# Three instructions reordered in an expert's closing sum, a ranking advanced by two steps, and an early load of a count

## The chip, the core and the metric

The kernel runs on one core of a Trainium2 chip. The core has five engines that each work through their own instructions in order: TensorE (PE in the profile; PEld is its weight load), VectorE (DVE), ScalarE (ACT), GpSimd (POOL) and SyncE (SP). They meet only at semaphores. SP and POOL issue most of the DMAs. The metric is the device time of one execution in microseconds (us); lower is better.

## The reference

One block of a hybrid decoder, on x of 1 x 4096 x 1024 in float32:

```python
h = rms_norm(x, attn_norm)
proj = h @ w_in                              # one projection for two groups of heads
o_a = gated_delta_net(...)                   # 4 heads, chunks of 64 tokens
o_b = retention(...)                         # 4 heads, chunks of 64 tokens
x = x + concat(o_a, o_b) @ w_out
h2 = rms_norm(x, ffn_norm)
x = x + hierarchical_moe(h2, ...)            # top 1 of 8 groups, then top 2 of its 8 experts
return rms_norm(x, final_norm)

# an expert, for the tokens routed to it (64 experts, hidden width 256):
y = (silu(t @ w_gate) * (t @ w_up)) @ w_down   # weighted by p(group) * p(expert | group)
```

Every token goes to two experts. Its row of the output is x plus both weighted results, normed with `final_norm`.

## The kernel before

The program has three stages. `mixer`, to about 2000 us, runs the projection and both groups of heads over eight blocks of 512 tokens. `post`, to about 2537 us, makes the output projection per block of 128 tokens (`Out.half`, L554 to L586), turns each finished block and routes its tokens (`turn_x`, and the generator `route`). The expert stage, 2537 to some 3470 us, runs the 64 experts.

The order of the instructions is that of the code: several generators are advanced in turns by hand. `side` is the list of side work in `post`. What stands in it there is `classes` (L1322 to L1370): from the counts of the first 28 of the 32 blocks it ranks the experts (VectorE, 64x64 tiles), so that the weights of the first four in the order can be fetched early. It yields between its steps: the counts (L1329, L1330), the groups' sizes (L1336 to L1344), their order (L1346 to L1354), the places (L1315 to L1318), a one-hot matrix `oh` (L1360 to L1364), and two small TensorE products with `oh` and `q` (L1367, L1368), whose results are `pe` and `br` (L1369, L1370). `turn_x` advances it by one step each time that a group of blocks has been handed to its routing; other places advance it too.

In the expert stage, round e of a Python loop runs the steps of several experts, in an order given as a string of letters, `LOOP = "AFCDNBEGIMHJLO"`; two rounds behind the last use `TAIL`. In a round, c is expert e, p the one before it (e-1) and q the one before that (e-2). The steps that matter here:

- F gathers for p the rows of the output that are so far there (`gather_y`, L1598, GpSimd's DMA).
- C and I are the gate and up matmuls of c (L1652), N the tanh of c (L1661, ACT).
- D is `sum_up` of q: for each of its tiles add (L1606, VectorE: `ys` plus the gathered row), square (L1611, ACT, which also sums over the row), rms (L1615 VectorE, L1616 GpSimd), gain (L1619, ACT: the row of `final_norm` times a flag of the token, plus 1).
- B and H turn the tiles of the next expert (L1582 TensorE, L1584 VectorE).
- E is silu of p: L1666 and L1667 (VectorE: `h`), L1668 (ACT: `hh`, the rounded high part), L1669 (VectorE: `hl`, the rest).
- G stores q: norm (L1623, L1624, VectorE, with the gain row `g`) and scatter (L1627, GpSimd's DMA).
- M scales the gathered rows of a later expert (L1575, ACT). J splits c's down weights into high and low parts (L1468 ACT, L1469 VectorE).
- O is the down projection of p: for each tile of up to 128 tokens two banks of 512 columns, six matmuls each (L975 to L977), each bank evicted by ACT into `ys` (L1595). The PSUM pool of these banks holds two, so the third bank of an expert with two tiles waits for the first eviction.

An expert has one tile or two, by its place in the order: 100 tiles in 64 experts. Flags and row numbers come from small tables (`mf`, `mi`). For a token's first expert the flag leaves the gain at 1, for its second it makes the final norm. A last loop, `For_i` over K (L1764), handles tokens beyond an expert's capacity; K is loaded into a register of five engines (L1763), and is 0 with these inputs.

The tiles `ys` and `g` (128 x 1024, float32) have two buffers each. The square's full-size result isn't used, only its sum; it is written into `g`, which gain then overwrites.

Of the kernel before, what the change touches and what calls it, by code (L numbers as in the profile page):

```python
# [8 lines left out]
F32 = mybir.dt.float32  # L9
# [3 lines left out]
AF = mybir.ActivationFunctionType  # L13
# [4 lines left out]
P = 128  # L18
D = 1024
# [9 lines left out]
NEXP, NGRP, EPG, DE = 64, 8, 8, 256  # L29
# [35 lines left out]
def pool(tc, ctx, name, bufs, **kw):  # L65
    return ctx.enter_context(tc.tile_pool(name=name, bufs=bufs, reuse_waits="tile", **kw))
# [845 lines left out]
NOV = 128  # L912
# [102 lines left out]
def post(tc, out, wrg, wre, sh, tab, then):  # L1015

    nc = tc.nc
    NR = out.x.shape[-2] // P
    with ExitStack() as ctx:
        cp, ap, sp = (pool(tc, ctx, n, b, side="right") for n, b in (("c1", 1), ("a1", 2), ("s1", 2)))  # L1020
# [12 lines left out]
        with tc.manual_schedule():  # L1033
            r0 = out.r
            if not out.mT:
                load_m(0)
                load_m(1)
                load_x(0)
                out.turn(0)
            load_x(r0 + 1)  # L1040

            back = [0, min(2 * r0, NR - NT)]
            xT, rst, scat, pend, side, again = [None], {}, [], [], [], {}
            turned = [0]

            def reload(end):
                while back[0] < min(back[1], end, turned[0] + 2):
                    r = back[0]
                    back[0] += 1
                    again[r] = y_row()  # L1050
                    nc.sync.dma_start(again[r], out.x1[r * P:(r + 1) * P, :])

            reload(r0)
            usb, oneb = (cp.tile([P, P], BF, name=n) for n in ("usb", "oneb"))
            oacc = cp.tile([P, 64], BF, name="oacc")
            nc.gpsimd.memset(oacc, 0.0)
            oaf = cp.tile([P, 64], F32, name="oaf")
            nc.gpsimd.memset(oaf, 0.0)
            sh.load()
            wrr = cp.tile([P, KC, 72], F32, name="wrr")  # L1060
            nc.sync.dma_start(wrr[:, :, 0:8], rows(wrg, 0, [[8, P], [P * 8, KC], [1, 8]]))
            nc.sync.dma_start(wrr[:, :, 8:72], rows(wre, 0, [[64, P], [P * 64, KC], [1, 64]]))
            load_m(r0 + 2)
            load_x(r0 + 2)
            wr = Split(cp.tile([P, KC, 72], F32R, name="wrh"), cp.tile([P, KC, 72], F32R, name="wrl"))

            def prepare():
                sh.prepare()
                yield
                nc.vector.tensor_copy(usb, C[:, C2_US:C2_US + P])  # L1070
                nc.vector.tensor_copy(oneb, C[:, C2_ONE:C2_ONE + P])
                for k in range(KC):
                    if k % 4 == 0:
                        yield
                    nc.vector.tensor_scalar(wrr[:, k], wrr[:, k], sh.pc[:, k:k + 1], None, op0=OP.mult)
                nc.scalar.activation(wr.hi, wrr, AF.Copy)
                yield
                nc.vector.tensor_tensor(wr.lo, wrr, wr.hi.bitcast(F32), op=OP.subtract)

            pend.append(prepare())  # L1080

            def on(gens):
                try:
                    return next(gens[0])
                except StopIteration:
                    gens.pop(0)

            def step():
                if pend:
                    on(pend)  # L1090
                if side and not older[0] in pend:
                    on(side)

            older = [None]

            def warm(n):

                t = out.ptr.tile([P, 4, P], F32, name="tr")
                for i in range(n):
                    nc.tensor.transpose(t[:, i % 4], sh.ident, sh.ident)  # L1100

            def turn_x(end):
                r = turned[0]
                if r >= end:
                    return
                turned[0] += 1
                i, sb = r % NT, r // NT
                if i == 0:
                    rst[sb] = [sp.tile([P, NT], F32, name=n) for n in ("ssq", "rst")]
                    xT[0] = Split(ap.tile([P, KC, T], F32R, name="xh", bufs=1), ap.tile([P, KC, T], F32R, name="xl", bufs=1))  # L1110
                if r < back[1]:
                    xi = again.pop(r)
                else:
                    xi = out.xi.pop(r)
                out.split_t(xi, xT[0].hi, xT[0].lo, slice(i * P, i * P + P))
                jx = ap.tile([P, D], BF, name="jx", bufs=1)
                nc.scalar.activation(jx, xi, AF.Square, accum_out=rst[sb][0][:, i:i + 1])
                reload(end)

                n = 2 if sb == NR // NT - 1 else NT  # L1120
                if (i + 1) % n == 0:

                    while pend and not (on(pend) and r == NR - 1):
                        pass
                    sl = slice(i + 1 - n, i + 1)
                    part = Split(*(t[:, :, sl.start * P:sl.stop * P] for t in (xT[0].hi, xT[0].lo)))
                    new = (route(tc, (r + 1 - n) * P, n, out.x.shape[-2], sh, (rst[sb][0][:, sl], rst[sb][1][:, sl]), part,
                                      wr, usb, oneb, oacc, oaf, tab, scat, (out.pacc, out.ptr, out.psm, sp)))
                    next(new)
                    while pend:  # L1130
                        on(pend)
                    pend.append(new)
                    if side:
                        on(side)
                    if sb == NR // NT - 2:
                        older[0] = new
                        side.append(classes(tc, sh, oneb, oacc, out.psm, sp))

            if NR == NT:
                side.append(classes(tc, sh, oneb, oacc, out.psm, sp))  # L1140
            for r in range(r0, NR):
                for i in out.half(r, 0):
                    if not i and r + 1 < NR:
                        out.turn(r + 1)
                    step()
                reload(r)
                for i in out.half(r, 1):
                    n = turned[0]
                    if not i or n < r:
                        turn_x(r)  # L1150
                    if n == turned[0] or turned[0] % NT and (turned[0] < NR - NT or turned[0] % 2):
                        step()
                load_m(r + 3)
                load_x(r + 3)
            while side:
                on(side)
            then()
            while turned[0] < NR:
                reload(NR)
                turn_x(NR)  # L1160
            on(pend)
            warm(40)
            while pend:
                on(pend)
            rank(tc, sh, oneb, oacc, out.psm, sp, warm)
            warm(140)
# [261 lines left out]
def moe(tc, w_gate, w_up, w_down, sh, x1, tab, info, out):  # L1428

    nc = tc.nc  # L1430
# [6 lines left out]
    with ExitStack() as ctx:  # L1437
        wp = pool(tc, ctx, "w2", 2)
        C, ident, pc, fn, ex, rk, pm, ovi = sh.C, sh.ident, sh.pc, sh.fn, sh.ex[:, 0:1], sh.rk, sh.pi, sh.ovi
# [50 lines left out]
        cp, ap, sp = (pool(tc, ctx, n, b) for n, b in (("c2", 1), ("a2", 2), ("s2", 2)))  # L1490
# [65 lines left out]
        class Rows:  # L1556
# [50 lines left out]

            def square(self):
                self.ss = sp.tile([P, 2], F32, name="ss2", bufs=4)
                self.g = ap.tile([P, D], F32, name="g")  # L1610
                nc.scalar.activation(self.g, self.xg, AF.Square, accum_out=self.ss[:, 0:1])  # L1611

            def rms(self):
                ss = self.ss
# [1 line left out]
                nc.gpsimd.tensor_tensor(ss[:, 1:2], ss[:, 0:1], ex, op=OP.pow)  # L1616

            def gain(self):
                nc.scalar.activation(self.g, fn, AF.Copy, scale=self.col(SEC), bias=1.0)  # L1619

            def norm(self):
# [72 lines left out]
        with tc.manual_schedule():  # L1694
# [23 lines left out]
            new(2)  # L1718
            X[1].each("scale")
            for e in range(NEXP + 2):  # L1720
                c, n, m, p, q = (X[i] if 0 <= i < len(X) else None for i in (e, e + 1, e + 2, e - 1, e - 2))
                if e % G == 0 and e + G < NEXP:
                    pend = table(batch(e + G))

                def sum_up():
                    for t in q.tiles:
                        t.add()
                        t.square()
                        t.rms()
                        t.gain()  # L1730

                def store():
                    for t in q.tiles:
# [24 lines left out]
                for o in LOOP if e < NEXP else TAIL:  # L1758
                    do, f = steps[o]
                    if do:  # L1760
                        f()

        K = nc.values_load(ovi[0:1, 2 * NOV:2 * NOV + 1], min_val=0, max_val=NOV)  # L1763
        with tc.For_i(0, K, 1) as j:  # L1764
            w = Weights(ovi[0:1, bass.ds(j, 1)])
            w.index()
# [18 lines left out]
            x.tanh()  # L1785
            x.silu()
            x.down()
            for f in ("gather_y", "add", "square", "rms", "gain", "norm", "scatter"):
                x.each(f)


# [49 lines left out]
```

## Time and profile before

| | |
|---|---|
| Three runs | 3479.33, 3486.98, 3489.43 us; median 3486.98 |
| Profiled execution | 3483.95 us, span 3482.0 us |
| Mean granted TensorE clock | 0.993 |
| TensorE busy (PE / weight loads) | 3382.3 us (97%) / 3102.6 us (89%) |
| VectorE busy | 2160.8 us (62%) |
| ACT busy | 1492.9 us (43%) |
| GpSimd busy | 1010.6 us (29%) |

The shares are means over three unlike stages. A row of an engine's timeline, as used below, reads: start, duration, engine, line, operation, result and inputs, how many such instructions in a row (x). A bracket at its end gives the idle time of the engine just before it and whom that waited for. Starts of neighbours may lie closer than a duration, since instructions overlap at their ends.

### The profile page before, as it was taken

To read this page: it belongs to the slowest core of one execution; us is meant where nothing else is said; L and a number is where in the kernel's file an instruction comes from. 1 tells how busy PE (TensorE), PEld (TensorE's weight loads), DVE (VectorE), ACT (ScalarE), POOL (GpSimd) and SP (SyncE) were. 2 spreads that over 40 slices of the span, in tenths; PEclk is the share of its full clock that TensorE was granted. 3 is DMA by queue.
4 is the path that set the end of the run, shared out by engine and by line. 5 is a ranking of instruction groups with operands and counts; after the bars stand their busy time and mean duration, and the time that the engine had idled before them with its cause. 6 is when DMAs were issued, how large, how long until landed. Compare 5 with 4: busy or idle time off the path is not lost. (4 is left out here: it accounts for less than half of the span.)

```text
span 3482.0 us, 65321 instructions
## 1 busy us (share of the span) xinstructions
PE 3382.3 (97%) x24377; PEld 3102.6 (89%) x24377; DVE 2160.8 (62%) x5718; ACT 1492.9 (43%) x3322; POOL 1010.6 (29%) x1320
## 2 busy tenths in 40 slices
PE   7999999999999999999999999999999999999996
PEld 6989999999999999999999988888888888888885
DVE  5785576576467566656655734444556677767775
ACT  4444243233333333333332323222255667766775
POOL 1322222232232322322222211111224344444543
PEclk9999999999999999999999999999999999999998
DMA  8675445454544545454554444323378898999995
GB/s 270 225 247 183 162 159 197 159 190 170 182 168 169 179 150 201 159 179 166 181 183 162 145 156 137 123 102 110 132 230 289 285 312 294 311 323 333 336 320 189
DMA packets 393422, 710.98 MB, mean 204 GB/s; under 512 B 52704, under 2 KB 272528, under 8 KB 393104
## 3 DMA queue, kind: packets, MB, share of 16 engines
q1 hardware_dynamic: 356736, 622.03, 52.6%
q0 software_dynamic: 34976, 84.20, 6.7%
q8 instruction: 193, 3.16, 0.4%
q14 instruction: 125, 1.02, 0.1%
q10 hardware_dynamic: 1392, 0.56, 0.1%
HBM read 606.19 MB, written 131.99 MB: 212 GB/s over the span
## 5 line engine op out<-in xcount | busy, mean ns | idle before, releaser
L248 PE MATMUL acc<-wq,hh 128*128 128x256 f32 (+1 forms) x2560 | 744.7, 291 | 16.6 <-DVE gs L281 6.8
L250 PE MATMUL acc<-wq,hl 128*128 128x256 f32 (+1 forms) x2560 | 722.4, 282 | 1.8 <-DVE hl L326 1.8
L249 PE MATMUL acc<-wq,hh 128*128 128x256 f32 (+1 forms) x2560 | 723.2, 283 | 0.2 <-DVE wq L145 0.2
L248 PEld LDWEIGHTS acc<-wq,hh 128*128 128x128 f32 x2560 | 486.2, 190 | 23.8 <-DVE gs L281 9.0
L250 PEld LDWEIGHTS acc<-wq,hl 128*128 128x128 f32 x2560 | 484.5, 189 | 2.6 <-DVE hl L326 2.6
L249 PEld LDWEIGHTS acc<-wq,hh 128*128 128x128 f32 x2560 | 486.1, 190 | 0.7 <-DVE wq L145 0.7
L236 PE MATMUL acc<-hh,wq 128*128 128x512 f32 x768 | 317.7, 414 | 0.0
L238 PE MATMUL acc<-hh,wq 128*128 128x512 f32 x768 | 301.6, 393 | 0.0
L237 PE MATMUL acc<-hl,wq 128*128 128x512 f32 x768 | 301.0, 392 | 0.0
L1652 PEld LDWEIGHTS g<-xT,gu 128*128 128x128 f32 x2048 | 270.3, 191 | 13.2 <-DVE xT L1584 3.4
L1652 PE MATMUL g<-xT,gu 128*128 128x128 f32 (+30 forms) x2048 | 275.6, 293 | 1.5 <-DVE xT L1584 1.5
L1652 PE MATMUL u<-xT,gu 128*128 128x128 f32 (+30 forms) x2048 | 275.6, 293 | 0.0
L1652 PEld LDWEIGHTS u<-xT,gu 128*128 128x128 f32 x2048 | 265.9, 191 | 1.9
L274 DVE SCALAR_TENSOR_TENSOR cv<-xin,pcol,cv 128x512 f32<-128x512 f32 x288 | 216.4, 751 | 73.4 <-ACT cv L272 66.6
L282 POOL TENSOR_TENSOR gs<-gs,nrow 128x256 f32<-128x256 f32 x128 | 98.1, 766 | 448.1 <-DVE gs L281 413.7
L1627 POOL DMA_INDIRECT out_dram<-xg,mi x100 | 130.8, 1308 | 189.0 <-DVE ss L1623 96.4
L975 PE MATMUL y<-dh,hh 128*128 128x512 f32 (+16 forms) x400 | 164.5, 411 | 21.7 <-ACT ys L1595 13.9
L1595 ACT ACTIVATE ys<-y,mf 128x512 f32<-128x512 f32 (+22 forms) x200 | 134.0, 681 | 115.8 <-PE y L977 115.1
L849 POOL TENSOR_TENSOR rqk<-rqk,rb 128x256 f32<-128x256 f32 x128 | 115.3, 901 | 222.6 <-DVE rb L848 132.3
L1598 POOL DMA_INDIRECT xg<-out_dram,mi x97 | 100.5, 1036 | 263.8 <-PE tr L1582 48.4
L238 PEld LDWEIGHTS acc<-hh,wq 128*128 128x128 f32 x768 | 144.2, 188 | 33.0
L291 POOL TENSOR_TENSOR ss<-ss,ex 128x2 f32<-128x2 f32 x128 | 101.4, 792 | 236.8 <-DVE ss L290 203.7
(377 smaller groups left out, 7942.4 us busy)
## 6 DMA issues: line engine op xcount, KB each, us to landing
wq<-wsp SPq DMA_DIRECT2D x420, 512.0 KB, 5.8
gu<-in_w_gate_dram SPq DMA_DIRECT2D x128, 512.0 KB, 6.4
gu<-in_w_up_dram SPq DMA_DIRECT2D x128, 512.0 KB, 7.9
dn<-in_w_down_dram SPq DMA_DIRECT2D x64, 1024.0 KB, 9.5
xi<-in_x_dram SPq DMA_DIRECT2D x64, 512.0 KB, 5.0
wsp<-wq SPq DMA_DIRECT2D x60, 512.0 KB, 4.4
mixed<-mx SPq DMA_DIRECT2D x128, 128.0 KB, 2.7
xi<-mixed SPq DMA_DIRECT2D x32, 512.0 KB, 4.7
```

Of the source, the lines that this page charges most:

```text
L236: nc.tensor.matmul(a, wh[:, s], hh[:, k, :], start=(k == 0), stop=False)
L237: nc.tensor.matmul(a, wh[:, s], hl[:, k, :], start=False, stop=False)
L238: nc.tensor.matmul(a, wl[:, s], hh[:, k, :], start=False, stop=(k == KC - 1))
L248: nc.tensor.matmul(a[:, :n], hh[:, k, s], wh[:, :n], start=(k == 0), stop=False)
L249: nc.tensor.matmul(a[:, :n], hh[:, k, s], wl[:, :n], start=False, stop=False)
L250: nc.tensor.matmul(a[:, :n], hl[:, k, s], wh[:, :n], start=False, stop=(k == KC - 1))
L274: nc.vector.scalar_tensor_tensor(cv, xin[:, j:j + T], tap(j), cv, op0=OP.mult, op1=OP.add)
L849: nc.gpsimd.tensor_tensor(o.rearrange("p h s d -> p (h s d)"), o.rearrange("p h s d -> p (h s d)"), b.rearrange("p h s d -> p (h s d)"), o ...
L975: nc.tensor.matmul(out, a.hi, b.hi, start=(i == 0), stop=False)
L1595: nc.scalar.activation(self.y[:R, s], y[:R], AF.Copy, scale=self.f[:R, WT, self.n:self.n + 1])
L1627: so = nc.gpsimd.indirect_dma_start(out=orow, out_offset=self.idx(0), in_=self.xg[:self.G], in_offset=None, bounds_check=S - 1, oob_is_err ...
L1652: nc.tensor.matmul(o[:, b, :R], self.w.gu[k // 4][:, k % 4, i * DE + b * P:i * DE + b * P + P], self.xT[:, k, :R], start=(k == 0), stop=(k ...
```

## The change

Four edits, with no instruction added or removed on any engine. `sum_up` runs gain first, then add, square and rms; the square writes its unused result into `ys` (`self.y`, already read by the add) rather than `g`. The load of K moves from behind the two tail rounds to the head of the first of them. `turn_x` advances `classes` by two steps where it advanced it by one.

```diff
@@ turn_x
                     pend.append(new)
-                    if side:
-                        on(side)
+                    for _ in range(2):
+                        if side:
+                            on(side)
@@ class Rows
             def square(self):
                 self.ss = sp.tile([P, 2], F32, name="ss2", bufs=4)
-                self.g = ap.tile([P, D], F32, name="g")
-                nc.scalar.activation(self.g, self.xg, AF.Square, accum_out=self.ss[:, 0:1])
+                nc.scalar.activation(self.y, self.xg, AF.Square, accum_out=self.ss[:, 0:1])
@@
             def gain(self):
+                self.g = ap.tile([P, D], F32, name="g")
                 nc.scalar.activation(self.g, fn, AF.Copy, scale=self.col(SEC), bias=1.0)
@@ the rounds of the experts
             for e in range(NEXP + 2):
+                if e == NEXP:
+                    K = nc.values_load(ovi[0:1, 2 * NOV:2 * NOV + 1], min_val=0, max_val=NOV)
@@
                 def sum_up():
                     for t in q.tiles:
+                        t.gain()
                         t.add()
                         t.square()
                         t.rms()
-                        t.gain()
@@ behind the rounds
-        K = nc.values_load(ovi[0:1, 2 * NOV:2 * NOV + 1], min_val=0, max_val=NOV)
         with tc.For_i(0, K, 1) as j:
@@ in that loop
-            for f in ("gather_y", "add", "square", "rms", "gain", "norm", "scatter"):
+            for f in ("gather_y", "gain", "add", "square", "rms", "norm", "scatter"):
                 x.each(f)
```

Line numbers behind the first edit are higher by one in the changed kernel up to the loop over the experts, except where the edits themselves shift them.

ACT in the expert stage, at the first `sum_up` with two tiles, before (`xg_29727` and `xg_29728` are the gathered rows of the two tiles, `fn` the row of `final_norm`):

```order
L1595 ACTIVATE ys<-y,mf 128x512 x4
L1611 ACTIVATE g,ss_30386<-xg_29727 128x1024
L1619 ACTIVATE g<-fn,mf 128x1024
L1611 ACTIVATE g,ss_30393<-xg_29728 128x1024
L1619 ACTIVATE g<-fn,mf 128x1024
L1661 ACTIVATE h<-g 128x2x76
L1668 ACTIVATE hh<-h 128x512
```

The same place of the changed kernel:

```order
L1596 ACTIVATE ys<-y,mf 128x512 x4
L1620 ACTIVATE g<-fn,mf 128x1024
L1611 ACTIVATE ys,ss_30388<-xg_29727 128x1024
L1620 ACTIVATE g<-fn,mf 128x1024
L1611 ACTIVATE ys,ss_30395<-xg_29728 128x1024
L1662 ACTIVATE h<-g 128x2x76
L1669 ACTIVATE hh<-h 128x512
```

Each gain (L1619, now L1620) went ahead of its tile's square; a square now stands last before the tanh.

TensorE near the end of `post`, before: the last output projection (L576 to L578), the two products of `classes` (`sm`), and the turn of the last block (`xi_28621`):

```order
L576 MATMUL acc<-hh,mh 128x512
L577 MATMUL acc<-hl,mh 128x512
L578 MATMUL acc<-hh,ml 128x512
L1367 MATMUL sm<-oh,cst_24670 128x64
L1368 MATMUL sm<-cst_24670,q 128x64
L554 MATMUL tr<-id,xi_28621 128x128 x8
```

In the changed kernel the products stand right behind the turn of the block before the last (`xi_28472`):

```order
L554 MATMUL tr<-id,xi_28472 128x128 x8
L1368 MATMUL sm<-oh,cst_24670 128x64
L1369 MATMUL sm<-cst_24670,q 128x64
L576 MATMUL acc<-hh,mh 128x512
L577 MATMUL acc<-hl,mh 128x512
L578 MATMUL acc<-hh,ml 128x512
```

Twelve matmuls (four times L576, L577, L578), which stood ahead of the products, now stand behind them.

GpSimd at the end of the tail, before: scatters of the last three tiles, the last gather, the load of K (`ovi`) and the loop's branch:

```order
L1627 DMA out_dram<-xg_29727,mi 4096x1024
L1598 DMA xg_29729<-out_dram,mi 96x1024
L1616 TENSOR_TENSOR ss_39730<-ss_39730,ex_24671 128x1
L1627 DMA out_dram<-xg_29728,mi 4096x1024
L1616 TENSOR_TENSOR ss_39759<-ss_39759,ex_24671 128x1
L1627 DMA out_dram<-xg_29729,mi 4096x1024
L1763 TENSOR_LOAD ovi
L1764 COMPARE_AND_BRANCH
```

The same place of the changed kernel:

```order
L1628 DMA out_dram<-xg_29727,mi 4096x1024
L1723 TENSOR_LOAD ovi
L1599 DMA xg_29729<-out_dram,mi 96x1024
L1616 TENSOR_TENSOR ss_39746<-ss_39746,ex_24671 128x1
L1628 DMA out_dram<-xg_29728,mi 4096x1024
L1616 TENSOR_TENSOR ss_39775<-ss_39775,ex_24671 128x1
L1628 DMA out_dram<-xg_29729,mi 4096x1024
L1766 COMPARE_AND_BRANCH
```

The load went ahead of one gather and two scatters.

## Rows read from the trace of the kernel before

**Rows 1.** Expert stage: length, then busy PE, PEld, DVE, ACT, POOL; clock, DMA share, GB/s.

```profile
2537.00:3482.00 945.00, 896.62 (x6100) 788.72 (x6098) 649.84 (x1288) 630.49 (x855) 400.89 (x394) 0.99 0.87 295
```

**Rows 2.** Waits in the expert stage, TensorE: us in total, times, longest.

```profile
PE y L975 <- ACT ys L1595: 13.9, 15, 1.5
PE y L975 <- ACT hh L1668: 7.8, 9, 2.1
```

**Rows 3.** The same view, of VectorE and ACT.

```profile
DVE ss L1615 <- ACT g L1611: 142.8, 100, 2.7
...
ACT g L1611 <- DVE xg L1606: 82.8, 75, 6.0
...
ACT hh L1668 <- DVE h L1667: 63.1, 62, 2.8
...
DVE xg L1606 <- DMA xg<-out_dram,mi: 1.6, 2, 1.1
```

**Rows 4.** ACT's timeline in the round at 2586: first square, second gain, tanh.

```profile
2586.05 1.05 ACT L1611 ACTIVATE g<-xg 128x1024 f32<-128x1024 f32 x1
...
2589.72 1.15 ACT L1619 ACTIVATE g<-fn,mf 128x1024 f32<-128x1024 f32 x1
2590.78 0.28 ACT L1661 ACTIVATE h<-g 128x152 f32<-128x152 f32 x1
```

**Rows 5.** ACT's timeline in the round at 3410: first square, and `hh`.

```profile
3410.47 1.06 ACT L1611 ACTIVATE g<-xg 128x1024 f32<-128x1024 f32 x1 [2.89 <-DVE xg L1606]
...
3416.07 0.42 ACT L1668 ACTIVATE hh<-h 128x260 fp32r<-128x260 f32 x1 [0.52 <-DVE h L1667]
```

**Rows 6.** ACT and TensorE in the round at 3368: square, first `ys`, third bank.

```profile
3368.16 1.04 ACT L1611 ACTIVATE g<-xg 128x1024 f32<-128x1024 f32 x1
...
3378.35 1.50 ACT L1595 ACTIVATE ys<-y,mf 128x512 f32<-128x512 f32 x2
...
3379.07 0.39 PE L975 MATMUL y<-dh,hh 128*4 128x512 f32 x1
```

**Rows 7.** ACT and TensorE in the round at 2586: `hh`, down, `ys`, third bank.

```profile
2592.16 0.63 ACT L1668 ACTIVATE hh<-h 128x512 fp32r<-128x512 f32 x1 [1.10 <-DVE h L1667]
...
2592.97 0.48 PE L975 MATMUL y<-dh,hh 128*128 128x512 f32 x1
...
2596.67 1.24 ACT L1595 ACTIVATE ys<-y,mf 128x512 f32<-128x512 f32 x2
...
2597.39 0.50 PE L975 MATMUL y<-dh,hh 128*128 128x512 f32 x1 [1.26 <-ACT ys L1595]
```

**Rows 8.** ACT and TensorE in the round at 3105: `hh` and down.

```profile
3111.22 0.40 ACT L1668 ACTIVATE hh<-h 128x236 fp32r<-128x236 f32 x1 [0.72 <-DVE h L1667]
...
3113.30 0.49 PE L975 MATMUL y<-dh,hh 128*118 128x512 f32 x1
```

**Rows 9.** VectorE near the end of `post`: a residual add, and `oh`.

```profile
2487.50 0.69 DVE L583 TENSOR_TENSOR xi<-acc,xi 128x512 f32<-128x512 f32 x1 [2.49 <-PE acc L578]
...
2501.70 0.24 DVE L1364 TENSOR_SCALAR oh<-cst,q 64x64 f32<-64x64 f32 x1
```

**Rows 10.** TensorE there: the products of `classes`, and the last block's turn.

```profile
2502.00 0.43 PE L1367 MATMUL sm<-oh,cst 64*128 64x64 f32 x2 [2.31 <-DVE oh L1364]
...
2502.58 1.09 PE L554 MATMUL tr<-id,xi 128*128 128x128 f32 x8
```

**Rows 11.** TensorE up to the first expert: a gap in the routing, the first turn.

```profile
2515.06 0.19 PE L1265 MATMUL sm<-ob,usb 128*128 128x64 bf16 x1 [1.08 <-DVE ob L1260]
...
2536.51 0.75 PE L1582 MATMUL tr<-cst,xg 76*128 76x76 f32 x8 [0.91 <-ACT xg L1575]
```

**Rows 12.** The granted clock (third number from the end) after two gaps, as rows 1.

```profile
2504.00:2506.00 2.00, 1.76 (x7) 1.47 (x8) 1.97 (x10) 1.40 (x3) 0.00 (x0) 0.50 0.58 190
...
2516.00:2520.00 4.00, 3.24 (x26) 2.83 (x25) 3.47 (x26) 3.75 (x4) 1.50 (x2) 1.00 1.10 352
```

**Rows 13.** GpSimd's load of K: duration in ns (min, median, max), first and last start.

```profile
L1763 POOLq TENSOR_LOAD <-ovi x1: 502/502/502, 3465.7 to 3465.7; - x1
```

## Prediction

> **What bounds the kernel now.** I read the busy time by stage first [rows 1]. The expert stage, 2537 to 3482 us, holds all that three of the four edits touch; TensorE is busy there for 896.62 of 945 us and ACT for 630.49. TensorE sets the pace, so an edit counts only where TensorE waits, or comes to wait. The waits of TensorE in that stage [rows 2] show for whom: the down projection (L975) waits 13.9 us in 15 places for `ys`, ACT's eviction, and 7.8 us in 9 places for `hh`, ACT's rounding of the hidden tile. So the moments at which ACT finishes `hh` and `ys` matter. Then the waits of the lines that the reorder moves [rows 3]: ACT sat 82.8 us before 75 of the 100 squares until VectorE's add was done; VectorE sat 142.8 us before `rms` until the square was done; ACT sat 63.1 us before 62 of the 64 `hh` until VectorE had `h`. That gives the chain of one round: add (VectorE), square (ACT), `rms` (VectorE), for a second tile the same again, then the turn, silu, `h` (VectorE), `hh` (ACT), down (TensorE). VectorE runs in order and `rms` waits for the square, so the square sits on the chain to `hh`; the gain doesn't.
>
> **The order gain, add, square, rms.** Nothing is added or taken away; per tile, one ACT instruction of 1.15 us goes ahead of the square. Its price as a place in ACT's row is 1.06 us, start of gain 2589.72 to start of the next 2590.78 [rows 4]; I use 1.05.
> Two kinds of rounds follow. In an early round ACT comes to the square before the add is done: 2.89 us of waiting at 3410.47 [rows 5]. The gain fits into that wait, and the square starts when it did. What does this buy? ACT is free 1.05 us sooner behind the last square, but its next instruction on the chain is `hh`, for which it waits anyway (0.52 us at 3416.07 for `h`). VectorE's chain has not moved, so nothing is gained. The gain of a second tile moves into the place where the first one's stood, between the two squares: no change either.
> In a late round the add has long been done, and ACT comes straight from the last `ys` eviction to the square: the one at 2586.05 has no wait [rows 4], the one at 3368.16 has none [rows 6]. There the gain now stands in the way: square, `rms`, turn, silu, `h` and `hh` all come up to 1.05 us later, and with `hh` all that ACT does behind it (scale, `dh`, `ys`). I went through the 62 rounds that have a square and a later `hh`, by ACT's wait before the first square: 29 are late, 20 with no wait and 9 with 0.16 to 0.91 us. The delays (1.05 less the wait) add up to 25.2 us. How much of it reaches TensorE is read from the down projection of each:
> - In the round at 2586, down starts at 2592.97, 0.18 us after `hh` (2592.16 + 0.63), and its third bank waits for `ys` from 2596.67 already (1.26 us, [rows 7]). Both move with ACT: full cost, 1.05. Four more are like it (2648, 2711, 2916, 2960): 5 x 1.05 = 5.25.
> - In the round at 3368 TensorE doesn't wait yet, but the third bank (3379.07) starts just when the first half of `ys` at 3378.35, 0.70 us long, is done [rows 6]: about 1.0. The round at 3297 is alike, and the one at 3034 has a delay of 0.82: 2.82.
> - At 2798 and 2900 `ys` has some 0.39 us to spare: 2 x 0.66 = 1.32. At 3019, 3338 and 3424 it is 0.17, 0.39 and 0.06: 0.62.
> - The other 16 cost nothing. Either the expert behind has one tile, so that no third bank is wanted, and down starts long after `hh`: at 3105 `hh` ends at 3111.62 and down starts at 3113.30 [rows 8], 1.68 us to spare. Or ACT waits over a microsecond for TensorE before its first `ys`, which swallows the delay.
> Sum 5.25 + 2.82 + 1.32 + 0.62 = 10.0 us. After each such round ACT waits for TensorE or meets an early round, so delays don't pile up. From below: if the spare times were all larger than the records say, 0; if ACT's freed microsecond did reach `hh` and `ys`, minus half of the 21.7 us in [rows 2], some 11 us gained. From above: all 25.2. I take 10.0 because it is read round by round.
>
> **The square into `ys`.** Same instruction, same size; `ys` has two buffers and is next written by ACT itself, in order. It only holds `ys` until the square, and the next eviction stands behind that on the same engine: 0.
>
> **The classes two steps at once.** VectorE's 64x64 ranking, ending in `oh`, stood between the routing steps of the last blocks; `oh` came at 2501.70 [rows 9], and TensorE sat 2.31 us for it at 2502.00 [rows 10]. Now the six instructions of the first step come while VectorE waits for the output projection (2.49 us idle before 2487.50), and the next steps run one place earlier each. Adding up the durations in the new order gives `oh` at about 2497.5. TensorE wants it earlier too, at 2496.7, ahead of twelve matmuls instead of behind them, and waits 0.8. Then 0.58 us for the small products (2502.00 to 2502.58), 12 x 0.23 for the matmuls, and the residual add (0.69 us at 2487.50) before the next block's turn: this starts at about 2501.8, and its first half perhaps at 2501.0, where it was 2502.58. So about 1.0 us (0.75 to 1.5). Behind it, up to the first expert at 2536.51 [rows 11], TensorE only waits for routing, tables and gathers, and the dummy transposes fill the time; a shift there goes through to the end.
> The clock adds to it. After the 2.31 us gap the granted clock is 0.50 in 2504 to 2506 [rows 12], the 1.2 GHz level: half of 2 us, 1.0 us of full speed is lost there. It stays low a little beyond, but TensorE also waits a little in this window, so I leave it at 1.0. After a gap of 1.08 us (2515.06, [rows 11]) the clock is 1.00 [rows 12]. The new gaps are no longer than that one, so I take the 1.0 as saved. The Trainium skill ("TensorE: Matmul & The Clock Gate", "What's actually happening") puts it thus: the throttled level is the default and activity releases it; the trace agrees so far as the low clock follows the longest gap. Together -2.0, bounds 0 to -2.6 (1.5 for the turn, 1.1 for the clock).
>
> **The load of K.** Five engines load the count. Four did so in the tail beside their own running work; SyncE's moves to the end of its queue, where nothing waits. GpSimd's load, 0.50 us [rows 13], stood with the last scatter at the end of the chain; now it stands ahead of the last gather, where GpSimd is idle. The scatter was queued first, so the chain may only seem to pass through the load: 0 to -0.5, I take -0.2. If TensorE's or VectorE's load weren't covered by the last rounds' work, up to 0.5 each is lost.
>
> **The sum.** +10.0 - 2.0 - 0.2 = +7.8 us. The profiled run took 3483.95 us, the median of the three is 3486.98; between the two, 3485.5 + 7.8 = 3493.3, so 3493.
>
> **The rivals.**
> - ACT's order doesn't matter: the delays vanish in spare time that the records understate (ends of matmuls are modelled). For it: 33 rounds have room. Against it: 15 places where TensorE already waits for `ys`. Time: 3485.5 - 2.2 = 3483. The Trainium skill ("Perfetto Trace Analysis", "Identifying the Most-Contended Engine") would have one work on the engine with the highest occupancy first, and ACT is not that one; by this rule the reorder is nothing. The waits in [rows 2] speak against it.
> - The freed microsecond counts: filling 75 waits lets ACT run ahead, and `hh` and `ys` come sooner. Against it: 62 of 64 `hh` wait for `h`. Time: 3485.5 - 11 - 2.2 = 3472.
> - The delay goes all through (slower by far): a late square makes norm and scatter late, the scatter holds back the next `gather_y`, and the add of an early round starts late in turn. It decides from the point at which most gathers land after the engines are ready. Against it: so far the add waited for a gather only twice, 1.6 us in all [rows 3]. Time: 3485.5 + 25.2 - 2.2 = 3508.
>
> **How the numbers follow.** Forecast 0.57, with a range of its own of 3487 to 3499 (reorder +4 to +14, the rest 0 to -3); order doesn't matter 0.20; freed microsecond 0.06; delay all through 0.17. 0.3% is 10.5 us, about what can be told from no change: the bounds are 3476.5 and 3497.5. Slower by more: a fifth of the forecast (0.11) and nearly all of the last case (0.16), 0.27. Faster by more: the third case, and a little for the second, 0.07. The rest 0.66. The range, 3480 to 3506, leaves out most of the third case and the far half of the last.
>
> **What would show it.** ACT's wait for the add before the square falls from 82.8 to about 43 (33 early rounds by 1.05 each, the nine partly late ones by 5 in all); VectorE's wait for the square grows from 142.8 by about 25; TensorE's waits for `ys` and `hh` grow from 21.7 to about 32. If VectorE's wait grows and TensorE's doesn't, the first rival holds; if both fall, the second; if TensorE's grow by 20 or more, the third. TensorE's wait for `oh` shows 0.8, the clock stays at 1.00, and the first expert's turn starts some 2 us before 2536.51. No load of K stands in the chain's end. I am wrong if the late squares don't start later.

## The result and the profile after

| | before | changed |
|---|---|---|
| six runs each, median | 3485.01 us | 3504.65 us |
| lowest to highest | 3479.33 to 3489.43 | 3500.07 to 3508.43 |
| span of the profiled execution | 3482.0 us | 3505.7 us |

The ratio is 1.0054 (95% interval 1.004 to 1.0068): slower by 18.8 us (13.9 to 23.7). The forecast was 3493, its range 3480 to 3506. The sign was right and the time lies in the range, 1.4 us below its upper end, but the loss is more than twice the +7.8 of the sum.

The waits in the expert stage, over the whole of it (us in total, times, longest), answer to [rows 2, 3]:

```profile
DVE ss L1615 <- ACT ys L1611: 166.5, 99, 3.6
ACT hh L1669 <- DVE h L1668: 120.6, 63, 2.8
...
ACT ys L1611 <- DVE xg L1607: 46.3, 59, 3.6
...
PE y L975 <- ACT ys L1596: 18.7, 18, 1.5
PE y L975 <- ACT hh L1669: 14.9, 14, 3.1
...
PE g L1653 <- DVE xT L1585: 2.5, 6, 0.7
...
DVE xg L1607 <- DMA xg<-out_dram,mi: 2.1, 4, 1.3
```

ACT's wait for the add fell from 82.8 to 46.3 us, as the gain now fills it (43 was forecast). VectorE's wait for the square grew by 23.7 us (25 forecast). TensorE's waits for `ys` and `hh` grew from 21.7 to 33.6 us (32 forecast). So the delay is where it was looked for, and of the size in those rows. Yet the time grew by more than these 11.9 us.

Where the rest is, one stretch shows: from the first to the last turn of the expert stage, before (first row) and after (second), columns as in rows 1.

```profile
2536.50:3437.40 900.90, 877.71 (x5972) 773.16 (x5973) 631.35 (x1258) 612.72 (x829) 390.31 (x383) 1.00 0.90 306
```

```profile
2536.70:3461.20 924.50, 888.01 (x5972) 777.60 (x5973) 630.15 (x1258) 601.08 (x830) 396.82 (x383) 0.99 0.88 298
```

Of the 23.7 us by which the profiled execution is longer, 23.6 are here. TensorE's idle time (length less busy) went from 23.2 to 36.5 us, +13.3. And with the same 5972 matmuls it was busy 10.3 us longer. Part of that is the clock: over these two stretches, the granted clock lost 1.7 us against full speed before, in one place (within 3096 to 3102), and 8.5 us after, in three (within 2539 to 2547, 3112 to 3117 and 3436 to 3445; the shares of full speed lost there are 0.43, 0.34 and 0.38). That is 6.8 us more. The other 3.5 us or so I can't assign: the ends of matmuls are modelled, and weight loads that wait may stretch them.

The late round of [rows 4, 7]: the last `ys` ahead of the first square, before, and ACT in the changed kernel:

```profile
2585.47 0.69 ACT L1595 ACTIVATE ys<-y,mf 128x512 f32<-128x512 f32 x1 [0.67 <-PE y L977]
```

```profile
2588.94 0.69 ACT L1596 ACTIVATE ys<-y,mf 128x512 f32<-128x512 f32 x1 [0.61 <-PE y L977]
2589.53 1.14 ACT L1620 ACTIVATE g<-fn,mf 128x1024 f32<-128x1024 f32 x1
2590.57 1.04 ACT L1611 ACTIVATE ys<-xg 128x1024 f32<-128x1024 f32 x1
2591.61 1.14 ACT L1620 ACTIVATE g<-fn,mf 128x1024 f32<-128x1024 f32 x1
2593.12 1.06 ACT L1611 ACTIVATE ys<-xg 128x1024 f32<-128x1024 f32 x1 [0.37 <-DVE xg L1607]
2594.18 0.28 ACT L1662 ACTIVATE h<-g 128x152 f32<-128x152 f32 x1
2596.73 0.63 ACT L1669 ACTIVATE hh<-h 128x512 fp32r<-128x512 f32 x1 [2.28 <-DVE h L1668]
```

and TensorE behind it:

```profile
2597.41 0.50 PE L975 MATMUL y<-dh,hh 128*128 128x512 f32 x1 [0.76 <-ACT hh L1669]
...
2601.96 0.50 PE L975 MATMUL y<-dh,hh 128*128 128x512 f32 x1 [1.26 <-ACT ys L1596]
```

From the start of the last `ys` to that of the first square it is 1.63 us, where it was 0.58 (2585.47 to 2586.05): 1.05 later, exactly the gain's place. ACT then waits 2.28 us for `h` (1.10 before): the time that the early gain took is handed back as a wait that no one can use. Down waits 0.76 us where it had 0.18 to spare. The wait for `ys` is as long as before, 1.26 us, but comes later.

The end of `post`, TensorE, answers to [rows 10, 11]: the turn of the last block but one and the dummy transposes (L1100), before, then the changed kernel:

```profile
2495.92 1.03 PE L554 MATMUL tr<-id,xi 128*128 128x128 f32 x8
...
2509.45 4.53 PE L1100 MATMUL tr<-cst 128*128 128x128 f32 x40
```

```profile
2498.05 1.03 PE L554 MATMUL tr<-id,xi 128*128 128x128 f32 x8
...
2499.67 0.43 PE L1368 MATMUL sm<-oh,cst 64*128 64x64 f32 x2 [0.59 <-DVE oh L1365]
...
2503.12 0.60 PE L554 MATMUL tr<-id,xi 128*128 128x128 f32 x4
2504.06 0.66 PE L554 MATMUL tr<-id,xi 128*128 128x128 f32 x4 [0.35 <-DVE xi L583]
...
2509.47 4.53 PE L1100 MATMUL tr<-cst 128*128 128x128 f32 x40
```

The wait for `oh` is 0.59 us (2.31 before, 0.8 forecast), and the last turn now waits for the residual add, as the sum had it. From the one to the other it is 11.42 us, where it was 13.53: 2.1 us saved. The clock, last columns of two windows:

```profile
2504.00:2506.00 2.00, 1.29 (x11) 0.96 (x12) 0.91 (x3) 1.53 (x3) 0.00 (x0) 1.00 0.58 211
2506.00:2508.00 2.00, 2.00 (x18) 2.00 (x18) 1.97 (x15) 0.59 (x2) 0.00 (x0) 1.00 0.89 265
```

It stays at 1.00 where it was 0.50 in the first of them. The first expert starts at 2536.65, and not some 2 us before 2536.51 as forecast: this execution came to the turn of the last block but one 2.1 us later (2498.05 against 2495.92), and had been as late at 2195 us already, ahead of every edit.

### The profile page after: what moved, and what is told of

Read it like the earlier page. It is cut to its first block, busy times and chain, and to the rows that moved or that the text cites. A ratio compares the mean times of both kernels' runs of the same rounds, so it can differ in the third digit from the quotient of the medians.

```text
span 3505.7 us, 65421 instructions
## 1 busy us (share of the span) xinstructions
PE 3396.0 (97%) x24377; PEld 3110.7 (89%) x24377; DVE 2159.7 (62%) x5718; ACT 1479.9 (42%) x3322; POOL 1016.7 (29%) x1320
## 5 line engine op out<-in xcount | busy, mean ns | idle before, releaser
L248 PEld LDWEIGHTS acc<-wq,hh 128*128 128x128 f32 x2560 | 487.8, 191 | 22.3 <-DVE gs L281 9.1
L975 PE MATMUL y<-dh,hh 128*128 128x512 f32 (+16 forms) x400 | 165.7, 414 | 33.6 <-ACT ys L1596 18.7
```

Of the source, the lines that this page charges most:

```text
L248: nc.tensor.matmul(a[:, :n], hh[:, k, s], wh[:, :n], start=(k == 0), stop=False)
L975: nc.tensor.matmul(out, a.hi, b.hi, start=(i == 0), stop=False)
```

## The experiments

Each was timed beside the kernel before, on the same chip; us are the ratio times the median of before beside it (3484.06 for the first four, 3490.84 for the next four, 3489.48 for the last two).

**Only the order.** All of the diff but the `turn_x` loop and the move of K. 

> Only the order of sum_up (gain first, square into ys); classes and K as before. Theory A, the late square: the whole loss of the change (+18.8 us) and the 1 to 2 us that the other edits were to give back come from here, so +14 to +21 us, TensorE's waits for ys and hh about 34 us as in the changed kernel (21.7 before). Rival B, the classes edit costs the rest (it moved a stretch of low clock to 2538-2546 us, 3.3 us lost): +8 to +12 us here.

Measured: 1.0052 (1.004 to 1.0064), +18.1 us (13.9 to 22.3). TensorE's waits for `ys` and `hh` are 32.1 us in its trace. The reorder, with its square into `ys`, is the whole loss; rival B falls.

**Only the classes.**

```diff
-                    if side:
-                        on(side)
+                    for _ in range(2):
+                        if side:
+                            on(side)
```

> Only the classes two steps at once. Theory A: -2 to 0 us against before. Rival B: +3 to +8 us, with a stretch of low clock in the first expert's up matmuls (2538 us on).

Measured: 0.9995 (0.9986 to 1.0003), -1.7 us (-4.9 to +1.0). That suits the forecast's -2.0, but alone it can't be told from no change. Its trace does have a stretch of low clock at the first expert (2534.6 to 2541.4 us), as rival B had it, and the time is none the worse. In nine of the twelve traces of this case some such stretch begins between 2534 and 2553 us: in all three kernels with this edit, in six of the nine without it. So it doesn't need the classes. What does go with them is the stretch that the prediction counted: in all nine traces without this edit a low clock begins between 2499 and 2520 us, in the three with it none does.

**Gain first for pairs alone, and for single tiles alone.** Both with the square into `ys`.

```diff
                     for t in q.tiles:
+                        if len(q.tiles) == 2:     # the other kernel: == 1
+                            t.gain()
                         t.add()
                         t.square()
                         t.rms()
-                        t.gain()
+                        if len(q.tiles) == 1:     # the other kernel: == 2
+                            t.gain()
```

Pairs: 

> Gain first only in the rounds whose sum has two tiles; single tiles as before. All 29 late rounds of the trace of before have two tiles. Theory A: the same time as with the whole reorder (+14 to +21), since all late rounds are in it. Rival C, what costs is something that every tile has (the buffer ys held longer, or the gain waiting for a free g): about 0.7 of it, 72 of 100 tiles.

Measured: 1.0056 (1.004 to 1.0071), +19.5 us (13.9 to 24.7), as the whole reorder.

Single tiles: 

> Gain first only in the 28 rounds whose sum has one tile. Theory A: none of them is late (ACT waited 1.33 us or more for the add in each), the gain fits into the wait, and nothing waits for it: within 2 us of before, ACT's wait for the add about 25 us shorter. Rival C: about 0.3 of the whole reorder, +4 to +6. Rival D, freed ACT time counts: -4 us or more.

Measured: 1.0007 (0.9999 to 1.0016), +2.4 us (-0.3 to +5.6). ACT's wait for the add is 51.2 us there, 32 shorter, and nothing is gained by it: rival D falls. Rival C's +4 to +6 lies partly within this interval; against it stands the kernel with pairs, which lost the whole (13.9 to 24.7) and not 0.7 of the 18.1, some 12.7. The loss sits in the pairs, where all the late rounds are.

**Gain first in 13 rounds, and in 16 others.** The 29 late rounds, split by what the prediction charged.

```diff
                 def sum_up():
+                    early = e - 2 in (1, 5, 9, 15, 22, 23, 26, 30, 31, 50, 53, 55, 59)
+                    # the other: (2, 6, 10, 13, 16, 18, 21, 24, 29, 32, 36, 42, 45, 48, 51, 56)
                     for t in q.tiles:
+                        if early:
+                            t.gain(True)          # allocates g
                         t.add()
-                        t.square()
+                        t.square(early)           # into ys, else into g
                         t.rms()
-                        t.gain()
+                        if not early:
+                            t.gain()
```

The 13: 

> Gain first (and the square into ys) only in the 13 rounds that the prediction charged. Theory A: what the trace of the order-only kernel shows for these rounds, +9.8 us, and near the +10.0 of the prediction's sum; with a clock that drops after longer waits up to +12. If the delay is paid elsewhere (rival E, the early rounds behind), under +6.

Measured: 1.0023 (1.0014 to 1.0033), +8.0 us (4.9 to 11.5). In its trace these 13 rounds, taken from the start of one up matmul to the next, are 9.7 us longer than before, and the 16 are 1.3. The interval alone would leave room for rival E's "under +6"; by the trace the 13 rounds pay themselves.

The 16: 

> Gain first only in the 16 late rounds that the prediction charged nothing. By the prediction: 0 (within 2 us). By theory A as the order-only trace has it: +5 to +8 us, since VectorE's xT and a slower clock behind longer waits make TensorE pay there too.

Measured: 1.0017 (1.0009 to 1.0026), +5.9 us (3.1 to 9.1). These rounds are not free. In this kernel's trace they are 3.0 us longer than before, nine of them by 0.1 to 0.7. In the order-only kernel they are 6.1 us longer, the 13 are 9.8, and the other 34 together 3.6: 19.5 in all. Sums like these differ between executions too: in the trace of the kernel with only the load of K moved, whose code is that of before in all these rounds, the 16 are 1.2 us longer, the 13 0.8 and the other 34 2.9. What TensorE waits for in one of the 16, the round with the square at 2601.23 before, in the timeline of the order-only kernel:

```profile
2615.57 6.53 PE L1652 MATMUL g<-xT,gu 128*128 128x232 f32 x32 [0.20 <-DVE xT L1584]
```

This is the next expert's gate matmul, waiting for VectorE's copy of the turned rows. Down had time to spare, as the prediction said; but the same VectorE does this copy behind the norm, and it starts 2.57 us after down, where it was 1.74. The waits of the gate's weight loads (PEld) for this copy, before, in the kernel with the 16 and in that with the 13:

```profile
PEld g L1652 <- DVE xT L1584: 3.4, 6, 1.3
```

```profile
PEld g L1655 <- DVE xT L1584: 7.9, 13, 0.9
```

```profile
PEld g L1655 <- DVE xT L1584: 3.3, 5, 1.2
```

Seven more places wait when the 16 are late, none when the 13 are.

Not all of the 6.1 us is of this kind. The round that was at 2844 has 2.6 of them in the order-only kernel, with a short wait and then a low clock, TensorE's timeline and the windows around it:

```profile
2856.62 0.48 PE L975 MATMUL y<-dh,hh 128*108 128x512 f32 x1 [0.66 <-ACT hh L1668]
...
2857.59 0.63 PE L975 MATMUL y<-dh,hh 128*108 128x512 f32 x1
```

```profile
2852.00:2856.00 4.00, 3.61 (x33) 3.18 (x31) 2.61 (x6) 1.87 (x4) 2.09 (x3) 1.00 0.80 294
2856.00:2860.00 4.00, 3.38 (x9) 2.45 (x10) 3.48 (x7) 3.82 (x5) 1.05 (x1) 0.64 1.08 322
```

Matmuls that took 0.39 us take 0.63; the low clock has some 1.7 of the 2.6 us. But this round's own order isn't the cause: with only the 16 reordered, this round among them, it is 0.1 us longer, and with only the 13, where it has the old order, 1.6. In all four kernels that reorder the 13 it is 1.6 to 2.6 longer, in the other seven -0.3 to 0.8. So most of it is handed on from earlier rounds, through GpSimd. VectorE's norm there, before and in the order-only kernel:

```profile
2834.04 0.27 DVE L1623 TENSOR_SCALAR ss<-ss,mf 128x1 f32<-128x1 f32 x1 [1.57 <-POOL ss L1616]
```

```profile
2843.30 0.27 DVE L1623 TENSOR_SCALAR ss<-ss,mf 128x1 f32<-128x1 f32 x1 [3.59 <-POOL ss L1615]
```

GpSimd's second half of `rms` stands behind its gather (L1598), which starts 10.59 us ahead of this round's up matmul where it was 12.56. So the norm waits 2.0 us longer, and the add behind it on VectorE comes 2.0 us later. What held the gather, these traces don't tell.

**Only the square into `ys`.** The old order.

```diff
             def square(self):
                 self.ss = sp.tile([P, 2], F32, name="ss2", bufs=4)
-                self.g = ap.tile([P, D], F32, name="g")
-                nc.scalar.activation(self.g, self.xg, AF.Square, accum_out=self.ss[:, 0:1])
+                nc.scalar.activation(self.y, self.xg, AF.Square, accum_out=self.ss[:, 0:1])
             def gain(self):
+                self.g = ap.tile([P, D], F32, name="g")
```

> Old order, only the square's unused result goes into ys instead of g. By the prediction: 0. Theory F, from the traces: the second square of a pair starts 2.62 us behind the first where it was 2.54, 0.08 us in each of 36 pairs, so +1 to +3 us, the same as the kernel with gain first in single tiles alone (+2.4) had.

Measured: 1.0004 (0.9996 to 1.0013), +1.4 us (-1.4 to +4.5): not to be told from nothing. But the 0.08 us is there. One pair of squares with the add between them:

```profile
3373.11 1.04 ACT L1610 ACTIVATE ys<-xg 128x1024 f32<-128x1024 f32 x1
...
3374.35 1.20 DVE L1606 TENSOR_TENSOR xg<-ys,xg 4x1024 f32<-4x1024 f32 x1
...
3375.72 1.06 ACT L1610 ACTIVATE ys<-xg 128x1024 f32<-128x1024 f32 x1 [0.43 <-DVE xg L1606]
```

2.61 us from square to square, where 3368.16 and 3370.68 of before are 2.52 apart. Over 36 pairs the median spacing is 2.54 us with the square into `g` and 2.61 to 2.62 in the kernels that write `ys` for pairs. Neither the square nor the add is longer: the median from the add's end to the second square's start went from 0.08 to 0.17 us. Why isn't shown.

**The other way round: grouped.** The square into `g` as before; for a pair, both adds, both squares, both rms, then both gains.

```diff
                 def sum_up():
-                    for t in q.tiles:
-                        t.add()
-                        t.square()
-                        t.rms()
-                        t.gain()
+                    for f in ("add", "square", "rms", "gain"):
+                        q.each(f)
```

> The other way round: for a pair of tiles all adds, then all squares, all rms, all gains (square into g as before). Theory A: the second square no longer waits for rms of the first and sits 1.3 us earlier on the chain to hh, while both gains fill ACT's wait for h; TensorE's 21.7 us of waits for ys and hh fall by 8 to 18 us, and the time by as much. Rival, TensorE's waits come from elsewhere (gathers, weights): within 3 us of before.

Measured: 0.9965 (0.9952 to 0.9978), -12.2 us (-16.8 to -7.7). ACT in the late round of [rows 4], then TensorE's waits:

```profile
2594.91 1.05 ACT L1611 ACTIVATE g<-xg 128x1024 f32<-128x1024 f32 x1
...
2596.31 1.06 ACT L1611 ACTIVATE g<-xg 128x1024 f32<-128x1024 f32 x1 [0.26 <-issue]
...
2597.36 2.17 ACT L1619 ACTIVATE g<-fn,mf 128x1024 f32<-128x1024 f32 x2
2599.44 0.28 ACT L1661 ACTIVATE h<-g 128x152 f32<-128x152 f32 x1
2600.56 0.63 ACT L1668 ACTIVATE hh<-h 128x512 fp32r<-128x512 f32 x1 [0.84 <-DVE h L1667]
```

```profile
PE y L975 <- ACT ys L1595: 10.6, 13, 1.5
PE y L975 <- ACT hh L1668: 2.2, 3, 1.1
```

From the first square to `hh` it is 5.65 us, against 6.11 before and 6.16 in the changed kernel, whose first square is itself 1.05 late. In the round at 3368, where the tiles are smaller, it is 4.73 against 5.88, but there the first square waits 0.72 us for the add, and from the last `ys` to `hh` it is 6.13 against 6.47. TensorE's waits fell from 21.7 to 12.8 us. The same view that shows the loss shows the gain, with the opposite sign. Two things changed at once, the second add ahead of the first `rms` and the gains behind both squares; which of them has how much of the gain wasn't tried.

**Only the load of K.**

```diff
             for e in range(NEXP + 2):
+                if e == NEXP:
+                    K = nc.values_load(ovi[0:1, 2 * NOV:2 * NOV + 1], min_val=0, max_val=NOV)
...
-        K = nc.values_load(ovi[0:1, 2 * NOV:2 * NOV + 1], min_val=0, max_val=NOV)
```

> Only the load of K moved to the head of the first tail round. Theory: GpSimd's load leaves the end, the chain behind the last norm is up to 0.5 us shorter and nothing else moves: -0.5 to 0 us, which five rounds can't tell from no change; its trace shows whether the last scatter starts sooner behind the last norm (0.30 us from the end of L1624's 1.28 us at 3464.36 to the scatter at 3465.94 before).

Measured: 1.0004 (0.9996 to 1.0013), +1.4 us (-1.4 to +4.5). Its last norm ends at 3473.25 (3471.97 + 1.28), its last scatter at 3474.50: 1.25 us. Before these were 3465.64 and 3466.89, also 1.25. The load left the chain in the profile and took no time with it.

**Grouped, with the classes and the load of K.** The three diffs together. 

> Grouped sum (adds, squares, rms, gains) with the classes two steps at once and the early load of K. Theory: the gain of the grouped order (-12 us) and that of the classes (-1 to -2 us) add up: -11 to -15 us, ahead of the grouped order alone by less than can be told. Rival: the earlier classes move the stretch of low clock into the first expert and eat their gain: as the grouped order alone or up to 3 us behind it.

Measured: 0.9954 (0.994 to 0.9968), median 3471.78 us against 3489.48: -16.1 us (-20.9 to -11.2). It beats both kernels of this case. Its lead over the grouped order alone is within both intervals, and so is the sum of the parts. The rival isn't excluded, as -12 lies in the interval; the stretch of low clock is at the first expert as it says (2535.5 to 2542.3 us).

## Why the prediction was right in sign and short in size

- The chain of a round (add, square, `rms`, turn, silu, `h`, `hh`, down) and the split into early and late rounds held: pairs alone carry the loss, single tiles don't.
- The 13 charged rounds: 10.0 us forecast, 9.8 in the trace of the order-only kernel, +8.0 when made alone. Round by round it held as well: +1.07 for the round at 2586, +1.13 and +1.12 for those at 2648 and 2711, 0.71 for 2798. The rounds at 2900, 3019 and 3424 cost nothing, and 3297 and 3368 a little more than said.
- The step that failed is "The other 16 cost nothing": +5.9 us (3.1 to 9.1) when made alone. I had looked at the one place where `hh` and `ys` are taken, down, and not followed VectorE's row on to the copy `xT`, for which the next expert's matmuls wait. In that kernel's trace these rounds are 3.0 us longer; where the rest of the +5.9 lies isn't shown. Of the 6.1 us that the same rounds are longer in the order-only kernel, 2.6 are one round with a low clock, late by what earlier rounds handed on: "delays don't pile up" failed there.
- The 13 and the 16 made alone add up to +13.9 us, the whole reorder is +18.1. The difference is within the intervals; the rest of this list has what may be in it.
- "No change" in early rounds: 3.6 us in the order-only trace over 34 rounds, but the kernel with only K moved has 2.9 there with no change in them; single tiles alone gave +2.4, not clear of noise. What part of it the 0.08 us per pair has, and what part the clock, stays open.
- The clock was in the sum for the end of `post` and not for the expert stage. There it falls after waits, short ones too, such as those ahead of 2857. The traces of before, order-only and changed kernel lost 1.7, 5.1 and 8.5 us to it in that stage. But the largest stretches, at the first experts, come and go between kernels without a link to an edit, so its share in the 18.8 us isn't settled. And the step by which the clock's 1.0 us in `post` was taken as saved, that new gaps no longer than 1.08 us would leave it at 1.00, came true in `post` and failed at the first expert, where it fell after waits of 1.01 and 0.30 us.
- The square into `ys` at 0: a small delay is there, its time not measurable. The classes: -2.0 forecast, 2.1 in the trace, -1.7 timed. K: -0.2 forecast, 0 found; the caution that "the chain may only seem to pass through the load" was right.
- The rivals: the first two are excluded by the sign. The third came nearest in time (3508), but mostly not by its mechanism. It rested on the gathers, and VectorE's add waited for them 2.1 us in 4 places where it had been 1.6 in 2. Only the round at 2844 has something of it, a gather that starts late and an add that is late for it. The delay went through in more rounds than the 13, by `xT` and by `hh`, and the clock added to it.
- That the time lies within the range is partly luck. Its upper end was put there for the near half of the third rival; the terms that were missing, `xT` and the clock in the expert stage, had no place in it.

## What to carry to other kernels

An in-order engine that waits is not free at the moment when another instruction is put ahead of the one that it waits for: it delays that one by up to its full length wherever the engine comes late, and fills a gap only where it comes early. Count both kinds of rounds, and put work that nobody waits for behind the instructions that the chain needs, as the grouped order puts the gains behind both squares. When a delay is followed through, follow it through every consumer of the late engine, and not only to the wait that the profile shows already.

## What the runs showed that I had not expected

The granted clock fell to its lower level (0.50, 1.2 GHz) in the midst of work that was dense: in the order-only kernel at 2857 us after waits of 0.19 and 0.66 us, with TensorE busy 3.61 of the 4 us up to 2856. At the first experts, in the changed kernel, it stood at 0.50 from 2540 to 2546 after two waits of 1.01 and 0.30 us, where the kernel before, with waits of 0.91 and 0.30 at the same place, kept 1.00. Single stretches lost 1.7 to 8.5 us against full speed, and all of one execution's in the expert stage, up to its last turn, 1.7 to 13.7 us; that they are much of why runs of one kernel lie 10 us apart is likely, but not shown. Writing an unused result into a tile that VectorE has just read delayed the second of two squares by 0.08 us.
